# Hybrid decoder layer on one core: small products of a projection slot regrouped, turned values in one tile, first slot's order changed

## The chip, the core and the metric

The kernel runs on one core of one Trainium2 chip. The core has a matrix engine (PE, with its weight loads shown apart as PEld), a vector engine (DVE), a scalar engine (ACT), a third elementwise engine (POOL), and a queue of its own from which most transfers are issued (SP). Products land in a small accumulator memory (PSUM) from which ACT and DVE fetch them. The metric is the device time of one execution in microseconds (us); smaller is better. Three executions of the kernel before took 992.99 us in the median, from 992.9 to 996.05.

## The reference, cut to what matters

One decoder layer over T = 528 rows (16 learned meta tokens and 512 tokens) of width 1024. One projection of the normalised input feeds two mixers with 16 heads of 64 channels each; their outputs are weighed by gates, added, projected, normalised, and go through a feed-forward stage of width 4096.

```
z = layer_norm(concat(meta_tokens, x))          # 528 x 1024
p = z @ w_in                                    # q, k, v of attention, r, k, v and three small inputs of RWKV-7, two gates
# sliding-window attention, 128 keys back, one sink per head, 8 query heads per key head
logits = q k^T / 8 + bias(distance), masked to the window
probs  = exp(logits - m) / (sum exp(logits - m) + exp(sink - m))
att    = probs v
# RWKV-7, per head, S is 64 x 64, step after step
a = sigmoid(a0 + al @ a2);  w = exp(-exp(w(wl)));  g = sigmoid(gl) @ g2
S = S * w_t + (S (-kk_t)) (kk_t a_t)^T + v_t k_t^T
y_t = S r_t
y = (group_norm(y) + bonus) * g
m = sigmoid(gate_a) * att + sigmoid(gate_r) * y
h = deepnorm(z, m @ w_out);  out = deepnorm(h, relu(h @ w1)^2 @ w2)
```

The outputs of the 16 meta rows are dropped at the end.

## The kernel before

**Dense products.** All matrices of weights are multiplied in three steps: the weights and the activations are each split into a high and a low part (ACT makes `whi` at L256, DVE makes `wlo` at L259), and the function `three` (L339 to L342) issues high by high, high by low and low by high into one accumulator bank, `dps`. One unit of dense work is a block of 128 columns of a weight matrix: for 8 blocks of input rows, these three steps, on 264 + 264 columns where all 528 rows are wanted, on 512 where the meta rows aren't. A unit's results are fetched by ACT and DVE (its `evict` function). These fetches run at a raised priority (`ahead(PRI["dense"])`) except inside an aside function that has its own.

**Slots.** The 16 heads are worked on in 8 pairs, and the projection in slots s = -1, 0, ..., 8. A slot holds the dense units of about one pair (names `q`, `k`, `r`, `v`, `ga`, `gr` with the pair's number: queries, keys, reads, values, gate of attention, gate of RWKV) and, between the dense steps, the small products of several pairs at different stages:

- `project_in(s+1)`: the small inputs of the next pair (`rwkv_begin`, `rwkv_lora` twice with accumulator `dps` of the pool `pat`, fetched by ACT at L500, scanned by DVE at L505; `rwkv_sums`, accumulator `ss`, L577).
- `scan(s)`: the pair's scores inside a chunk of 64 steps (`rwkv_scores`, `sc`, L668), the triangular inverse in blocks of 16 on DVE (`rwkv_inverse`, L773 and L777 alternating 15 times, then the copy `Xr` at L778, through DRAM and back as `X` and `XB`), and the transposes (`rwkv_turn_scores`, `rwkv_turn_keys` L729, `rwkv_turn_values` L746).
- `solve(s-1)`: the inverse put together from its blocks (`up` at L820, four levels), folded (`wp` L871, `gq`), the chain of states over 8 chunks (`ch` L946, `Z` on DVE and ACT at L904 and L906), the outputs `Y` (L960) and their norm.
- `attend(s-1)` and `join(s-1)`: the pair's attention, with `sp` (scores, L1131), a softmax on DVE and ACT over `sb`, `pt` (the probabilities transposed, L1169), `av` (L1189), the gate `ga` (L1195), and the sum of both mixers (`merge`).

All of these small products are plain fp32, the dense ones are not. **What sets the order.** The function `weave` walks a list of items `(due time, needs, function)` in order of due time and issues dense steps until the due time has come; the clock of the due times is a count of the dense steps' model durations. So the lists in `scan`, `solve`, `project_in`, `attend` and `join` fix PE's order row by row. The order on DVE, ACT, POOL and SP is set by a scheduler with static priorities at build time, which `ahead(n)` raises for what stands inside it; on the chip each engine runs its own list in order. The accumulator memory is given out as 8 banks: 2 for `dps` of the dense units, 2 of pool `pg` (`sc`, `bp`, `wp`, `gq`, `axt`, `tr`, `vt`, and `ss`), 2 of `pat` (the lora's `dps`, `sp`, `gp`, `pt`, `av`), and one each for `ch` and `Y`. A product that opens a bank waits until the bank's last user has been fetched.

After slot 8 the output projection (L1282 to L1284) and the feed-forward stage (`dps` on 512 columns up, L1501 to L1503 down) follow; the change doesn't touch them.

## Time and profile before

| what | before |
| --- | --- |
| median of three executions | 992.99 us (992.9 to 996.05) |
| profiled execution, its own time | 996.54 us |
| its span in the profile | 994.7 us |
| PE busy | 949.3 us, 95% of the span |
| PEld busy | 790.0 us, 79% |
| DVE busy | 653.1 us, 66% |
| ACT busy | 468.8 us, 47% |
| POOL busy | 44.2 us, 4% |
| mean granted PE clock in the slots | 0.97 to 1.00 |

The span is what the profile records; the execution's own time holds 1.8 us more around it. The profile is one execution, its rows are instructions or groups of them, and a row in square brackets tells how long the engine had stood idle before and what ended that. The count of a group is that of the chip's instructions: a plain fp32 product of the program is two or more of them there. In the trace slot 1 begins at about 114.0 us, slot 2 at 179.5, slot 3 at 243.6, slot 4 at 307.7, and the last slot has ended at 636.

### The profile page before, as it was taken

The page shows a single profiled execution, that of the slowest core. Times are in us where ns is not written, and L with a number is a line of the kernel's source. Part 1 is how long each engine was busy: PE and PEld are TensorE (multiplying, and loading weights), DVE is VectorE, ACT ScalarE, POOL GpSimd, SP SyncE. Part 2 cuts the span into 40 slices and gives each one's busy share as a digit, 9 for nine tenths or more (in the row PEclk, how much of TensorE's full clock was granted, in tenths as well). Part 3 has the DMA queues.
Part 4 walks back from the last instruction along what each step waited for, and adds up shares of the span by engine and source line. Part 5 has one row for each costly group of instructions (what it writes and reads, how often), then busy time and mean ns, then how long its engine had stood idle before and what let it go on. Part 6 is the DMA issues. An engine that isn't in the chain of part 4 may idle for free.

```text
span 994.7 us, 19253 instructions
## 1 busy us (share of the span) xinstructions
PE 949.3 (95%) x7557; PEld 790.0 (79%) x7557; DVE 653.1 (66%) x1505; ACT 468.8 (47%) x1226; POOL 44.2 (4%) x108
## 2 busy tenths in 40 slices
PE   4989899999999999999999999999999999999996
PEld 3989788888888887878886777888888888888885
DVE  8577698787887878778867866766433235443427
ACT  6535448455584575745836833743422224342220
POOL 2000000010010000100001001000000000000001
PEclk9999999999999999999999999999999999999999
DMA  7444432433224432233443536233222232223232
GB/s 270 94 126 120 105 80 69 125 76 105 75 50 123 100 118 68 70 108 88 128 127 103 162 118 229 68 106 116 95 89 102 88 104 88 103 85 106 71 100 84
DMA packets 82674, 105.47 MB, mean 106 GB/s; under 512 B 47766, under 2 KB 54664, under 8 KB 82584
## 3 DMA queue, kind: packets, MB, share of 16 engines
q1 hardware_dynamic: 81088, 102.16, 34.8%
q10 hardware_dynamic: 1496, 2.08, 0.6%
q8 instruction: 59, 0.97, 0.4%
q14 instruction: 31, 0.25, 0.1%
HBM read 86.29 MB, written 13.74 MB: 101 GB/s over the span
## 4 chain that ended last, share of the span: by engine, by line
PE 67%; DVE 17%; ACT 9%; DMA 3%; issue 2%; POOL 0%; SPq 0%; DVEq 0%; ACTq 0%; POOLq 0%
PE dps L340 12%; PE dps L341 11%; PE dps L342 11%; PE acc L1501 6%; PE acc L1503 6%; PE acc L1502 6%; DVE wlo L259 2%; ACT Z L753 2%; PE sc L668 2%; PE av L1189 2%; DVE AX L893 2%; PE o L1282 1%; DVE ftmp L773 1%; DVE Xf L777 1%; PE o L1284 1%
## 5 line engine op out<-in xcount | busy, mean ns | idle before, releaser
L259 DVE TENSOR_TENSOR wlo<-wraw,whi 128x512 fp32r<-128x512 f32 x240 | 158.0, 684 | 176.2 <-ACT whi L256 175.7
L256 ACT CAST whi<-wraw 128x512 fp32r<-128x512 f32 x240 | 140.7, 617 | 275.1 <-PE dps L341 130.6
L340 PE MATMUL dps<-hhi,whi 128*128 128x264 f32 (+1 forms) x640 | 219.3, 343 | 2.5 <-ACT whi L256 1.1
L341 PE MATMUL dps<-hlo,whi 128*128 128x264 f32 (+1 forms) x640 | 205.4, 321 | 1.4 <-DVE hlo L321 1.4
L342 PE MATMUL dps<-hhi,wlo 128*128 128x264 f32 (+1 forms) x640 | 204.2, 319 | 0.4 <-DVE wlo L259 0.4
L340 PEld LDWEIGHTS dps<-hhi,whi 128*128 128x128 f32 x640 | 122.0, 191 | 16.4 <-issue 2.0
L342 PEld LDWEIGHTS dps<-hhi,wlo 128*128 128x128 f32 x640 | 121.8, 190 | 9.1 <-DVE wlo L259 0.6
L341 PEld LDWEIGHTS dps<-hlo,whi 128*128 128x128 f32 x640 | 121.9, 190 | 6.8 <-DVE hlo L321 2.5
L341 PE MATMUL dps<-h1lo,whi 128*128 128x512 f32 (+1 forms) x256 | 97.5, 381 | 0.0
L340 PE MATMUL dps<-h1hi,whi 128*128 128x512 f32 (+1 forms) x256 | 97.4, 381 | 0.0
L342 PE MATMUL dps<-h1hi,wlo 128*128 128x512 f32 (+1 forms) x256 | 97.4, 381 | 0.0
L342 PEld LDWEIGHTS dps<-h1hi,wlo 128*128 128x128 f32 x256 | 48.1, 188 | 10.1
L340 PEld LDWEIGHTS dps<-h1hi,whi 128*128 128x128 f32 x256 | 48.1, 188 | 10.0
L341 PEld LDWEIGHTS dps<-h1lo,whi 128*128 128x128 f32 x256 | 48.1, 188 | 10.0
L1502 PE MATMUL acc<-wlo,hhi 128*128 128x512 f32 x128 | 50.5, 395 | 0.0
L1501 PE MATMUL acc<-whi,hhi 128*128 128x512 f32 x128 | 50.5, 395 | 0.0
L1503 PE MATMUL acc<-whi,hlo 128*128 128x512 f32 x128 | 50.1, 392 | 0.0
L1503 PE MATMUL acc<-whi,flo 128*128 128x512 f32 x112 | 44.0, 393 | 0.0
L1501 PE MATMUL acc<-whi,fhi 128*128 128x512 f32 x112 | 44.0, 393 | 0.0
L1502 PE MATMUL acc<-wlo,fhi 128*128 128x512 f32 x112 | 43.6, 390 | 0.0
L906 ACT ACTIVATE Z<-ch,PC 64x64 f32<-64x64 f32 x56 | 17.3, 309 | 44.8 <-DVE Z L904 43.5
L1601 DVE TENSOR_TENSOR rl<-rl 128x512 f32<-128x512 f32 (+1 forms) x36 | 22.8, 632 | 15.4 <-ACT hhi L1600 9.2
(302 smaller groups left out, 1746.6 us busy)
## 6 DMA issues: line engine op xcount, KB each, us to landing
wraw<-in_w_ff_dram SPq DMA_DIRECT2D x64, 512.0 KB, 3.5
wraw<-in_w_in_dram SPq DMA_DIRECT2D x52, 512.0 KB, 4.1
wraw<-in_w_out_dram SPq DMA_DIRECT2D x8, 512.0 KB, 4.0
xt<-in_x_dram SPq DMA_DIRECT2D x4, 512.0 KB
Nd<-NT SPq DMA_DIRECT2D x16, 128.0 KB, 2.8
bv<-bv SPq DMA_DIRECT2D x8, 256.0 KB
bvm<-bv SPq DMA_DIRECT2D x8, 256.0 KB, 3.7
qs<-qhi SPq DMA_DIRECT2D x16, 128.0 KB, 4.3
```

The lines of the kernel that those rows point to most:

```text
L256: act.copy(hi[:n, qs], raw[:n, qs])
L259: dve.tensor_tensor(lo[:n, qs], raw[:n, qs], hi[:n, qs].bitcast(F32), op=ALU.subtract)
L340: pe.matmul(ps, whi, xhi, start=first, stop=False)
L341: pe.matmul(ps, whi, xlo, start=False, stop=False)
L342: pe.matmul(ps, wlo, xhi, start=False, stop=last)
L668: pe.matmul(scs[e][:, c * P : (c + 1) * P], BK[ER[e], 4 * i + c, :], AXg[ER[e], e, 4 * i + c], start=True, stop=True,)
L753: act.copy(Z[2 * i + cc][64 * (1 - e) : 64 * (1 - e) + 64, e, :], vt[64 * cc : 64 * cc + 64, i * P + e * HD : i * P + (e + 1) * HD],)
L893: dve.tensor_tensor(AXg[:, e, cs], AXg[:, e, cs], gqs[e].rearrange("p (c k t) -> p c k t", c=4, k=2), op=ALU.add,)
L1501: pe.matmul(acc[b], xhi[k][:, bs], hi[:, ws], start=first, stop=False)
L1502: pe.matmul(acc[b], xhi[k][:, bs], lo[:, ws], start=False, stop=False)
L1503: pe.matmul(acc[b], xlo[k][:, bs], hi[:, ws], start=False, stop=last)
L1601: dve.tensor_tensor(r, r, r, op=ALU.mult)
```

## The change

- **Turned values.** `Z` was 8 tiles, filled by 16 copies of 64x64 on ACT in each `rwkv_turn_values`. It is now one tile with the 8 chunks as slices, filled by 4 copies of 64x256.
- **Bank of the sums.** `ss` is opened in pool `pat` and no longer in `pg`.
- **Grouping.** Due times are set so that small products which stood between dense steps each by themselves stand side by side: the sums and the keys' transposes with the outputs (18.6), the values' transposes with the norm (23.2), the lora at 7.4 and 8.6, and the second half of a pair's attention (`attention_turn`, `attention_out`, now in `attend_out`), with the last addition of `merge`, no longer at the end of the slot (26.0 to 31.5) but at the front of the next one (0.0, 4.6, 6.4, 7.0) beside the inverse's products. The product `gp` of the RWKV gate is no part of its dense unit any more but an item (`gate_out`, 11.6), and `merge` is cut in two (`merge_rwkv` at 25.4, `merge`).
- **Priority of fetches.** The queries' fetches (`qhi`, `qlo`) stand inside `ahead(PRI["dense"])`. In slot 0 the inverse's steps on DVE stand inside `ahead(PRI["up"])`.
- **Order of units.** In slot 0 the queries go ahead of the next pair's keys. In slots 1 to 6 the RWKV gate goes ahead of the attention gate. In slot 7 the order becomes RWKV gate, queries, attention gate, and the last two gates.

```diff
...
 AHEAD = 2
-NBUF = {'AX': 2, 'BK': 1, 'NT': 2, 'GR': 2, 'Z': 8}
+NBUF = {'AX': 2, 'BK': 1, 'NT': 2, 'GR': 2}
...
         pool.memset(dvm, 1.0)
-        ss = pg.tile([P, 512], F32, name="ss", tag="g")
+        ss = pat.tile([P, 512], F32, name="ss", tag="a")
...
         v = S["v"]
-        Z = [rw.tile([P, 2, HD], F32, name=f"Z{c}", tag="Z", bufs=NBUF["Z"]) for c in range(NCH)]
-        S["Z"] = Z
+        Z = rw.tile([P, NCH, 2, HD], F32, name="Z", tag="Z")
+        S["Z"] = [Z[:, c] for c in range(NCH)]
...
                 )
-            for i in range(4):
-                for cc in range(2):
-                    for e in range(2):
-                        act.copy(
-                            Z[2 * i + cc][64 * (1 - e) : 64 * (1 - e) + 64, e, :],
-                            vt[64 * cc : 64 * cc + 64, i * P + e * HD : i * P + (e + 1) * HD],
-                        )
+            v4 = vt.rearrange("p (i e h) -> p e i h", i=4, e=2)
+            for cc in range(2):
+                for e in range(2):
+                    act.copy(
+                        Z[64 * (1 - e) : 64 * (1 - e) + 64, cc::2, e, :],
+                        v4[64 * cc : 64 * cc + 64, e],
+                    )
...
         pool.memset(Xf.rearrange("p a b -> p (a b)")[:, 0 :: B + 1], 1.0)
-        for s in range(B - 1):
-            nj, nt = s + 1, B - 1 - s
-            tv = tmp[:, 0 : nj * nt].rearrange("p (j t) -> p j t", j=nj)
-            dve.tensor_tensor(
-                tv, Xf[:, 0:nj, s : s + 1].to_broadcast([NB, nj, nt]),
-                Nf[:, s : s + 1, s + 1 :].to_broadcast([NB, nj, nt]), op=ALU.mult,
-            )
-            dve.tensor_tensor(Xf[:, 0:nj, s + 1 :], Xf[:, 0:nj, s + 1 :], tv, op=ALU.add)
-        dve.tensor_copy(Xr, Xf[0:64].rearrange("p a b -> p b a"))
+        with ahead(PRI["up"] if j == 0 else 0):
+            for s in range(B - 1):
+                nj, nt = s + 1, B - 1 - s
+                tv = tmp[:, 0 : nj * nt].rearrange("p (j t) -> p j t", j=nj)
+                dve.tensor_tensor(
+                    tv, Xf[:, 0:nj, s : s + 1].to_broadcast([NB, nj, nt]),
+                    Nf[:, s : s + 1, s + 1 :].to_broadcast([NB, nj, nt]), op=ALU.mult,
+                )
+                dve.tensor_tensor(Xf[:, 0:nj, s + 1 :], Xf[:, 0:nj, s + 1 :], tv, op=ALU.add)
+            dve.tensor_copy(Xr, Xf[0:64].rearrange("p a b -> p b a"))
...
         def evict(ps, t0, n):
-            act.activation(hi, ps, AF.Copy, scale=HD**-0.5)
-            dve.scalar_tensor_tensor(
-                lo, ps, HD**-0.5, hi.bitcast(F32), op0=ALU.mult, op1=ALU.subtract
-            )
+            with ahead(PRI["dense"]):
+                act.activation(hi, ps, AF.Copy, scale=HD**-0.5)
+                dve.scalar_tensor_tensor(
+                    lo, ps, HD**-0.5, hi.bitcast(F32), op0=ALU.mult, op1=ALU.subtract
+                )
...
+        A["gw", j] = gwh, gwl
         yield from dense(COL_GRW + j * P, XT_, evict)
+    def gate_out(j):
         gp = pat.tile([P, 512], F32, name="gp", tag="a")
-        three(gp, gwh, gwl, sghi, sglo)
+        three(gp, *A["gw", j], sghi, sglo)
...
         dve.scalar_tensor_tensor(t, t, 1.0, gp, op0=ALU.add, op1=ALU.mult)
-        yield 0.7
...
-    def merge(j):
+    def merge_rwkv(j):
...
         dve.tensor_tensor(z, z, A["gg", j], op=ALU.mult)
+    def merge(j):
+        z = SS[j]["z"]
...
     unit("av", COL_AV, aside_value())
+    query(0)
...
     reads(1)
-    query(0)
...
     for j in range(1, PAIRS - 1):
+        gate_rwkv(j - 1)
         gate_att(j - 1)
-        gate_rwkv(j - 1)
...
     j = PAIRS - 1
+    gate_rwkv(j - 1)
+    query(j)
     gate_att(j - 1)
-    query(j)
-    gate_rwkv(j - 1)
...
             (12.4, (), F(rwkv_turn_scores, j)),
-            (19.0, (), F(rwkv_turn_keys, j)),
+            (18.6, (), F(rwkv_turn_keys, j)),
             (16.0, (), F(rwkv_inverse_place, j)),
-            (21.4, (), F(rwkv_turn_values, j)),
+            (23.2, (), F(rwkv_turn_values, j)),
...
             (18.6, (), F(rwkv_outputs, j)),
-            (24.5, (), F(rwkv_norm, j)),
+            (23.2, (), F(rwkv_norm, j)),
...
             (0.0, (), F(rwkv_begin, j)),
-            (5.6, (), F(rwkv_lora, j, 0)),
-            (7.4, (), F(rwkv_lora, j, 1)),
-            (20.4, (f"k{j}",), F(rwkv_sums, j)),
+            (7.4, (), F(rwkv_lora, j, 0)),
+            (8.6, (), F(rwkv_lora, j, 1)),
+            (25.5 if j == 1 else 18.6, (f"k{j}",), F(rwkv_sums, j)),
...
-    def attend(j, t0=9.2, t1=26.0):
+    def attend(j, t0):
+        return [(t0, (f"q{j}",), F(attention_scores, j, 0))] + [
+            (t0 + t, (), F(attention_scores, j, 1 + i)) for i, t in enumerate((0.0, 2.8, 4.4))
+        ]
+    def attend_out(j, t0, t1, t2):
         return [
-            (t0, (f"q{j}",), F(attention_scores, j, 0)),
-            (t0, (), F(attention_scores, j, 1)),
-            (t0 + 2.8, (), F(attention_scores, j, 2)),
-            (t0 + 4.4, (), F(attention_scores, j, 3)),
-            (t1, (), F(attention_turn, j, 0)),
-            (t1 + 2.4, (), F(attention_out, j, 0)),
-            (t1 + 2.4, (), F(attention_turn, j, 1)),
-            (t1 + 4.8, (f"ga{j}",), F(attention_out, j, 1)),
+            (t0, (), F(attention_turn, j, 0)),
+            (t1, (), F(attention_out, j, 0)),
+            (t1, (), F(attention_turn, j, 1)),
+            (t2, (f"ga{j}",), F(attention_out, j, 1)),
...
-    def join(j, t2):
-        return [(t2, (f"gr{j}",), F(merge, j))]
+    def join(j, t0, t1, t2):
+        return [
+            (t0, (f"gr{j}",), F(gate_out, j)), (t1, (), F(merge_rwkv, j)), (t2, (), F(merge, j)),
+        ]
...
             if 0 < s < PAIRS - 1:
-                items += attend(s - 1) + join(s - 1, 31.5)
+                items += attend(s - 1, 9.2) + join(s - 1, 11.6, 25.4, 0)[:2]
+            if 1 < s < PAIRS:
+                items += attend_out(s - 2, 0.0, 4.6, 6.4) + join(s - 2, 0, 0, 7.0)[2:]
...
                 items += [(10.0, (), merged_before)]
-                items += attend(s - 1, t1=20.5) + join(s - 1, 26.5)
-                items += attend(s, 16.5)[:4]
+                items += attend(s - 1, 10.0) + attend_out(s - 1, 20.5, 22.9, 25.3)
+                items += join(s - 1, 11.6, 26.5, 26.5)
+                items += attend(s, 16.5)
...
             if s == PAIRS:
-                items += attend(s - 1, t1=3.0)[4:] + join(s - 1, 25.5)
+                items += attend_out(s - 1, 3.0, 5.4, 7.8) + join(s - 1, 0.0, 24.5, 25.5)
...
                 items += [(3.0 + 3 * b, (), F(residual_rows, b)) for b in range(4)]
```

**PE, the outputs in slot 2** (slots 1 to 6 alike; `dps` are the dense steps, `Y` the outputs, `tr` the transposed keys, `ss` the sums of the next pair). Before:

```order
L960 MATMUL Y<-Z_2098,AX 64x64
L960 MATMUL Y<-Z_2099,AX 64x64
L340 MATMUL dps<-hhi,whi 128x264
L341 MATMUL dps<-hlo,whi 128x264
L342 MATMUL dps<-hhi,wlo 128x264
L729 MATMUL tr<-con,BK 128x128 x8
L340 MATMUL dps<-hhi,whi 128x264
```

Now:

```order
L962 MATMUL Y<-Z,AX 64x64 x16
L729 MATMUL tr<-con,BK 128x128 x8
L577 MATMUL ss<-con,sq 64x2 x8
L578 MATMUL ss<-con,sq 16x2
L340 MATMUL dps<-hhi,whi 128x264
L341 MATMUL dps<-hlo,whi 128x264
L342 MATMUL dps<-hhi,wlo 128x264
```

The dense steps between `Y` and `tr` stand behind them now, and `ss`, which stood between dense steps of its own, follows `tr` at once.

**DVE, the front of slot 3** (`L` is the scan of the next pair's decay, `WT` the folded matrix, `Xf` and `ftmp` the steps of the inverse, `ga` and `z` the gate on attention and the sum of the mixers). Before:

```order
L611 TENSOR_TENSOR bv<-bp,v 128x512
L259 TENSOR_TENSOR wlo<-wraw,whi 128x512
L505 SCALAR_TENSOR_TENSOR L<-con,tw 128x528
L875 TENSOR_TENSOR WT<-wp,dv 128x512 x2
L773 TENSOR_TENSOR ftmp<-Xf,Nf 66x15
L777 TENSOR_TENSOR Xf<-Xf,ftmp 66x15
```

Now:

```order
L877 TENSOR_TENSOR WT<-wp,dv 128x512
L779 TENSOR_TENSOR Xf<-Xf,ftmp 66x15
L775 TENSOR_TENSOR ftmp<-Xf,Nf 66x28
L1200 SCALAR_TENSOR_TENSOR ga<-ga,av 128x512
L779 TENSOR_TENSOR Xf<-Xf,ftmp 66x2x14
L1215 TENSOR_TENSOR z<-z,ga 128x512
L775 TENSOR_TENSOR ftmp<-Xf,Nf 66x39
L779 TENSOR_TENSOR Xf<-Xf,ftmp 66x3x13
L775 TENSOR_TENSOR ftmp<-Xf,Nf 66x48
L779 TENSOR_TENSOR Xf<-Xf,ftmp 66x4x12
L775 TENSOR_TENSOR ftmp<-Xf,Nf 66x55
L505 SCALAR_TENSOR_TENSOR L<-con,tw 128x528
```

The scan `L`, which stood ahead of `WT` and of the inverse, stands behind `WT`, the first steps of the inverse, and `ga` and `z`. These two belong to the pair before, and stood at the end of the slot before.

**DVE, the inverse of pair 0 in slot 0** (`BK`, `u` are operands of the pair's scores). Before:

```order
L777 TENSOR_TENSOR Xf<-Xf,ftmp 66x11x5
L554 TENSOR_TENSOR BK<-kp,iP 64x8x64
L773 TENSOR_TENSOR ftmp<-Xf,Nf 66x48
L554 TENSOR_TENSOR BK<-kp,iP 64x8x64
L777 TENSOR_TENSOR Xf<-Xf,ftmp 66x12x4
L540 SCALAR_TENSOR_TENSOR u<-ta,k 128x528
L773 TENSOR_TENSOR ftmp<-Xf,Nf 66x39
L550 SCALAR_TENSOR_TENSOR BK<-u,drv,iP 64x8x64
L777 TENSOR_TENSOR Xf<-Xf,ftmp 66x13x3
```

Now:

```order
L775 TENSOR_TENSOR ftmp<-Xf,Nf 66x55
L779 TENSOR_TENSOR Xf<-Xf,ftmp 66x11x5
L775 TENSOR_TENSOR ftmp<-Xf,Nf 66x48
L779 TENSOR_TENSOR Xf<-Xf,ftmp 66x12x4
L775 TENSOR_TENSOR ftmp<-Xf,Nf 66x39
L779 TENSOR_TENSOR Xf<-Xf,ftmp 66x13x3
```

The steps of the inverse follow each other now; the products of other work that stood between them come later.

## The prediction

> **What bounds the kernel now.** I read the page first, then the table by stage, then what PE waits for, then PE's timeline around the small products. The page has PE busy for 95% of the span:
>
> ```profile
> span 994.7 us, 19253 instructions
> PE 949.3 (95%) x7557; PEld 790.0 (79%) x7557; DVE 653.1 (66%) x1505; ACT 468.8 (47%) x1226; POOL 44.2 (4%) x108
> ```
>
> So there is room for 45 us at most without making PE's own work shorter. The table by stage (window, length, then the busy time of PE, PEld, DVE, ACT, POOL, the granted clock, the DMA share, GB/s) shows one middle slot and the feed-forward stage:
>
> ```profile
> 243.60:307.70 64.10, 62.74 (x692) 52.83 (x695) 51.69 (x138) 38.45 (x117) 3.92 (x10) 1.00 0.34 94
> 636.00:994.00 358.00, 350.75 (x1585) 287.29 (x1583) 160.78 (x250) 110.19 (x202) 3.69 (x4) 1.00 0.28 93
> ```
>
> A slot lasts 64.1 us, PE is idle for 1.4 of them, and DVE for 12.4. The last 358 us hold no line of the change; I leave them as they are. What the change can move is PE's idle time in the slots, and what PE loses when it passes from dense steps to small products and back, which the profile books as busy. The waits of PE that it touches (total, times, mean):
>
> ```profile
> PE av L1189 <- DVE pown L1175: 4.9, 5, 1.0
> PE up L820 <- DMA X<-Xr: 3.6, 1, 3.6
> PE pt L1169 <- ACT sb L1159: 1.5, 1, 1.5
> PE sc L668 <- DVE AX L685: 1.1, 2, 0.6
> PE axt L708 <- DVE Xf L777: 0.7, 3, 0.2
> ```
>
> **The change part by part. A, fewer passages.** PE's timeline in slot 3 (start, duration) shows a lone `ch`, and `Y` and `tr` with dense steps between them:
>
> ```profile
> 280.02 0.28 PE L342 MATMUL dps<-hhi,wlo 128*128 128x264 f32 x1
> 280.24 0.34 PE L946 MATMUL ch<-Z,AX 128*64 128x64 f32 x4
> 280.50 0.39 PE L340 MATMUL dps<-hhi,whi 128*128 128x264 f32 x1
> 280.73 0.28 PE L341 MATMUL dps<-hlo,whi 128*128 128x264 f32 x1
> ...
> 281.58 0.28 PE L342 MATMUL dps<-hhi,wlo 128*128 128x264 f32 x1
> 281.79 1.15 PE L960 MATMUL Y<-Z,AX 128*64 128x64 f32 x32
> 282.87 0.39 PE L340 MATMUL dps<-hhi,whi 128*128 128x264 f32 x1
> 283.10 0.29 PE L341 MATMUL dps<-hlo,whi 128*128 128x264 f32 x1
> 283.22 0.29 PE L342 MATMUL dps<-hhi,wlo 128*128 128x264 f32 x1
> 283.35 1.03 PE L729 MATMUL tr<-con,BK 128*128 128x128 f32 x8
> 284.14 0.37 PE L340 MATMUL dps<-hhi,whi 128*128 128x264 f32 x1
> 284.34 0.28 PE L341 MATMUL dps<-hlo,whi 128*128 128x264 f32 x1
> ```
>
> Dense steps start 0.12 us apart (283.10 to 283.22). From the step before `ch` to `ch` it is 0.22, so entering costs 0.10; from the step behind it to the next 0.23, so leaving costs 0.11: 0.21 in all. For `Y` the same reading gives 0.09 and 0.11, for `tr` 0.01 and 0.08, together 0.29. In slot 7 these two stand side by side already, between steps of 512 columns (0.12 x 512/264 = 0.23 apart):
>
> ```profile
> 540.70 0.40 PE L342 MATMUL dps<-hhi,wlo 128*128 128x512 f32 x1
> 541.03 1.15 PE L960 MATMUL Y<-Z,AX 128*64 128x64 f32 x32
> ...
> 542.96 0.48 PE L340 MATMUL dps<-hhi,whi 128*128 128x512 f32 x1
> 543.28 0.39 PE L341 MATMUL dps<-hlo,whi 128*128 128x512 f32 x1
> ```
>
> Entering costs 0.10, leaving 0.09, and the two products take 1.93 (541.03 to 542.96) against 1.08 + 0.79 = 1.87 apart. So joining them saved 0.29 - 0.19 - 0.06 = 0.04. In the order of PE's instructions, stretches of plain fp32 products between dense steps fall from 181 to 152, by 29. Each is worth 0.04 (a whole-array transpose beside a narrow product) to 0.21 (a stretch like `ch` that vanishes into its like, as the two loras do, or `av` beside the narrow products of the inverse): -1.2 to -6.1 us. Both kinds are there in about equal number, so I take the middle, 0.13 each: **-3.8**.
>
> [...]
>
> **B and C, the attention's second half.** `av` followed its `pt` so closely at the slot's end that `pown`, made by DVE from `pt`, came late five times: 4.9 us. In the new order the first `av` has 27 dense steps between it and `pt`, over 3 us at 0.12 each, and the second has nine dense steps and other products; the mean wait is 1.0. I take the wait as gone: **-4.9** (0 to -4.9; without that cover it comes back at the front). The one wait of `pt` for `sb` in slot 6 goes the same way, since `pt` now comes in the slot after `sb`: **-1.5** (0 to -1.5).
>
> **D, the seam from slot 0 to slot 1.** DVE's, SP's and PE's timelines there:
>
> ```profile
> 105.47 0.38 DVE L778 COPY Xr<-Xf 64x256 f32<-64x256 f32 x1
> 108.27 0.59 SPq L781 DMA_DIRECT2D Xr<-Xr  x1
> 110.32 0.63 SPq L790 DMA_DIRECT2D X<-Xr  x1
> 113.32 0.73 PE L820 MATMUL up<-X,NT 16*32 16x16 f32 x64 [3.63 <-DMA X<-Xr]
> ```
>
> The copy is done at 105.85, but its transfer is issued only at 108.27, behind the queries' transfers on SP; from there to `up` it takes 5.05 (113.32 - 108.27). PE was ready at 113.32 - 3.63 = 109.69. With the queries a unit earlier, their transfers are out before, so even with the copy unmoved `up` could start at 110.9, a wait of 1.2. With the inverse's steps in one piece on DVE the copy comes some us earlier still, and the wait is gone: -3.6. What these steps now push back on DVE are the operands of pair 0's scores; a late `AX` cost `sc` 1.1 us in its two waits, and I charge that once: **-2.5** (0 to -3.6).
>
> **E.** `axt` waits three times, 0.2 each, until DVE's list has passed a step of the inverse; the attention's products now stand ahead of it on PE and give DVE that time: **-0.7** (0 to -0.7).
>
> **F, the copies of `Z`.** ACT's groups (busy, mean ns):
>
> ```profile
> L753 ACT COPY Z<-vt 64x64 f32<-64x64 f32 x128 | 26.4, 206 | 9.0 <-PE vt L746 7.6
> L733 ACT COPY GR<-tr 64x256 f32<-64x256 f32 x32 | 11.7, 364 | 1.3 <-PE tr L729 1.2
> ```
>
> The 32 new copies have the size of the `GR` copies: 11.7 us where 26.4 were. These 14.7 us lie on an engine that is busy for 47%, beside dense steps; nobody waits for `Z` until the next slot's chain. With that cover gone (a dense fetch queued behind it on ACT) it would be up to -1. I take **0** (0 to -1).
>
> **G, a new wait at the front of slots 2 to 6.** These stand now behind the attention's half. The rows of slot 3 before, DVE, ACT and PE:
>
> ```profile
> 259.25 1.26 DVE L505 TENSOR_TENSOR_SCAN L<-con,tw 128x528 f32<-128x528 f32 x1 [0.63 <-ACT tw L503]
> 260.43 1.26 DVE L875 TENSOR_TENSOR WT<-wp,dv 128x512 f32<-128x512 f32 x2
> 260.54 0.22 ACT L512 ACTIVATE Pm<-L 128x16 f32<-128x16 f32 x1 [1.32 <-DVE L L505]
> 261.91 0.84 ACT L500 ACTIVATE ta<-dps,drv 128x264 f32<-128x264 f32 x2
> 264.66 0.28 PE L1131 MATMUL sp<-khi,qs 128*128 128x256 f32 x1
> 298.99 0.44 PE L1189 MATMUL av<-pown,vdif 128*64 128x128 f32 x4 [0.97 <-DVE pown L1175]
> ...
> 299.80 0.44 PE L1169 MATMUL pt<-con,sb 128*128 128x128 f32 x2
> ```
>
> Twelve products of `av` take 0.81 (298.99 to 299.80), so both halves of 16 take 2.2, and the two `pt` about 1.0 more by the same pace: 3.2 us move ahead of `sp`, which comes to 264.66 + 3.2 = 267.9. `sp` opens a bank of `pat` that the second lora's first half holds until ACT has made `ta`, and `ta` stands behind `Pm`, `Px` and `iP` on ACT, which wait for the scan `L`. The lora is due 1.8 us later and 3.2 us of work stand ahead of it: `L` would start at 264.25. But DVE's list now has `ga` and `z` ahead of `L`, each of the size of one `WT` (0.63): it starts at about 265.5 and ends 1.26 later, at 266.75. `ta` began 1.4 behind the end of `L` (260.51 to 261.91), and its first half takes 0.42: the bank is free at 268.6, and PE waits 0.7, in each of five slots: **+3.5**. Were DVE on time it is 0; with one scan's duration (1.3) more, for instance behind a late `ftmp`, it is 2.0 x 5 = +10. Behind `sp` on PE everything of the slot is queued, so nothing gives this back. I take 0.7, the reading by rows.
>
> **H, slot 7.** The queries come second there, so their transfers stand behind the inverse's two on SP, 0.59 and 0.63 in the rows under D, and the scores of pair 6 or 7 may wait for them: **+1.2** (0 to +5, a wait like that of D with its 5.05 queue).
>
> The sum: -3.8 - 4.9 - 1.5 - 2.5 - 0.7 + 0 + 3.5 + 1.2 = **-8.7**. The profiled execution took 996.54 (its span 994.7 and 1.8 around it), so it would become 987.8. It was 3.5 us above the median of the runs, 992.99, whose own spread to the slowest run is 3.1. I take the difference off the median: **984.3 us**.
>
> **The rivals.** *No new wait:* the ends of A (-6.1) and D (-3.6) with B, C and E, and G and H at 0: -16.8, 976.2 us. For it: DVE has 12.4 us idle in a slot, and the scheduler may leave `L` enough room. Against it: DVE's order puts `ga` and `z` right before `L`.
>
> *Joining is worth nothing:* each stretch saves 0.04, as in slot 7, A is -1.2, the rest stands: -6.1, 986.9 us. For it: slot 7, the one place where the profile shows a joined stretch. Against it: the loras join their like.
>
> *Slower, by the chain at the front:* `L` (1.26), the exponentials (1.4) and `ta` (0.42) lie bare, 3.1 us in five slots, +15.5 instead of +3.5: 996.3 us. It decides from (8.7 + 3.5)/5 = 2.4 us of wait in a slot. For it: steps of three engines in a row, and two banks of `pat`; against it: dense steps stand between, and DVE would have to be 2.4 us later than read.
>
> *The waits only move:* `av` then waits at the front as it did at the end, `pt` too, and the seam waits for another transfer: B, C and D are 0 and the sum is +0.2, 993.2 us. Against it: the cover under B.
>
> **How the numbers follow.** Forecast 0.46, with its own range of 980 to 989; no new wait 0.20; joining worth nothing 0.17; slower 0.09; waits only move 0.08. About 0.3%, 3 us, is what a measurement of this kernel tells from no change, so faster ends at 990 and slower begins at 996. Faster: 0.45 + 0.20 + 0.16 = 0.81; slower 0.06 of the third rival and 0.01 of the last; the rest, 0.12, is the same. The range from 975 to 992 holds the forecast, the first two rivals nearly whole, and leaves out most of the last two.
>
> **What would show it.** A: PE's busy time in a slot like 243.6 to 307.7 falls by about 0.6 with its count of passages; if it falls by 0.2, joining is worth nothing. B, C: no row of `av` waiting for `pown`, none of `pt` for `sb`. D: no wait of `up` for `X`, or a row of `sc` in its place. G: a new row of `sp` waiting for ACT's `ta`, five times 0.7; if it is missing, the first rival, if it is above 2.4, the third. H: in slot 7 a wait of `sp` for the transfer `qs`. The forecast is wrong if the slots' period stays at 64.1 us.

## The result and the profile after

The changed kernel takes **984.34 us** in the median of four runs (983.99 to 987.41), the kernel before 993.61 on the same chip; the ratio is 0.9903, with a 95% interval from 0.9882 to 0.9924. The number of the forecast, 984.3, was met, and it lay in the range. Its sum was not met: two of its largest terms were wrong, and the largest single cause of the gain stood in it at nothing. The experiments found that out.

The page of the changed kernel (span, and busy time of each engine):

```profile
span 982.3 us, 19147 instructions
PE 940.8 (96%) x7557; PEld 787.7 (80%) x7557; DVE 655.2 (67%) x1505; ACT 455.7 (46%) x1130; POOL 47.8 (5%) x108
```

What PE waits for in it (total, times, longest; the third figure of the prediction's list is the longest wait too):

```profile
PE ch L948 <- ACT Z L908: 3.4, 5, 1.4
PE dps L340 <- DVE qlo L1072: 2.8, 6, 0.5
PE sp L1136 <- ACT ta L500: 2.7, 4, 0.7
PE vp L1052 <- ACT ta L500: 1.5, 1, 1.5
PE sp L1136 <- DVE sb L1139: 1.2, 1, 1.2
PE sc L668 <- DVE AX L685: 1.0, 2, 0.6
PE pt L1174 <- ACT sb L1164: 0.4, 1, 0.4
```

The waits of `av` for `pown` (4.9), of `up` for `X` (3.6) and of `axt` are gone. `sp` waits for `ta` as the forecast read it, 0.67 in four slots, and in slot 5 `vp` stands in its place with 1.47. In slot 1 `vp` waits another 1.47, for which the profile names no engine. A wait that no step of the forecast had is new: a dense step at the end of each of six slots waits 0.48 for `qlo`, where before there was one of 0.4.

The table by stage of the change, a middle slot and slot 7, in the columns of the prediction's table:

```profile
231.20:294.60 63.40, 62.24 (x687) 53.12 (x688) 51.84 (x138) 36.68 (x105) 4.28 (x10) 1.00 0.33 92
487.30:548.90 61.60, 58.51 (x621) 45.66 (x620) 48.02 (x127) 33.69 (x99) 2.86 (x3) 1.00 0.45 126
```

A middle slot takes 63.40 instead of 64.10. Slot 7, from its first `up` to the next, grew from 59.1 to 61.6, because the second half of one more pair's attention stands in it; slot 1 has that half less.

### The profile page after: what moved, and what is told of

Read it like the earlier page. It is cut to its first block, busy times and chain, and to the rows that moved or that the text cites. A ratio compares the mean times of both kernels' runs of the same rounds, so it can differ in the third digit from the quotient of the medians.

```text
span 982.3 us, 19147 instructions
## 1 busy us (share of the span) xinstructions
PE 940.8 (96%) x7557; PEld 787.7 (80%) x7557; DVE 655.2 (67%) x1505; ACT 455.7 (46%) x1130; POOL 47.8 (5%) x108
## 4 chain that ended last, share of the span: by engine, by line
PE 72%; DVE 17%; ACT 4%; DMA 2%; issue 2%; POOL 2%; SPq 0%; DVEq 0%; ACTq 0%
PE dps L340 12%; PE dps L341 11%; PE dps L342 11%; PE acc L1516 6%; PE acc L1518 6%; PE acc L1517 6%; DVE wlo L259 3%; PE sc L668 2%; PE o L1290 1%; PE av L1194 1%; PE ch L948 1%; PE wp L873 1%; PE o L1291 1%; PE o L1292 1%; POOL grs L971 1%
## 5 line engine op out<-in xcount | busy, mean ns | idle before, releaser
L340 PE MATMUL dps<-hhi,whi 128*128 128x264 f32 (+1 forms) x640 | 216.5, 338 | 4.5 <-DVE qlo L1072 2.8
L342 PE MATMUL dps<-hhi,wlo 128*128 128x264 f32 (+1 forms) x640 | 203.0, 317 | 0.4 <-DVE wlo L259 0.4
L340 PEld LDWEIGHTS dps<-hhi,whi 128*128 128x128 f32 x640 | 120.5, 188 | 19.4 <-DVE qlo L1072 4.1
L342 PEld LDWEIGHTS dps<-hhi,wlo 128*128 128x128 f32 x640 | 120.5, 188 | 9.0 <-DVE wlo L259 0.6
L340 PE MATMUL dps<-h1hi,whi 128*128 128x512 f32 (+1 forms) x256 | 97.5, 381 | 0.0
L342 PE MATMUL dps<-h1hi,wlo 128*128 128x512 f32 (+1 forms) x256 | 97.5, 381 | 0.0
L342 PEld LDWEIGHTS dps<-h1hi,wlo 128*128 128x128 f32 x256 | 48.1, 188 | 10.3
L340 PEld LDWEIGHTS dps<-h1hi,whi 128*128 128x128 f32 x256 | 48.1, 188 | 10.1
L908 ACT ACTIVATE Z<-ch,PC 64x64 f32<-64x64 f32 x56 | 17.3, 310 | 36.4 <-DVE Z L906 35.7
```

Of the source, the lines that this page charges most:

```text
L340: pe.matmul(ps, whi, xhi, start=first, stop=False)
L342: pe.matmul(ps, wlo, xhi, start=False, stop=last)
L908: act.activation(dst, src[ER[e]], AF.Copy, scale=scale)
```

## The experiments

Twelve more runs were made, one of them of the kernel before, in four groups on several chips; each has the kernel before beside it on its own chip, with medians of 996.1 to 997.4 there. The change itself ran only beside the 993.6 of its own chip, so rows of different groups are compared by their ratios. "Waits" is the sum of all listed waits of PE that end between 60 and 640 us, and "dips" is the time lost to a lower granted clock in the same stretch (last section but one); both are from the one profiled execution.

| kernel | median us | ratio to before (95%) | middle slot | waits | dips |
| --- | --- | --- | --- | --- | --- |
| before, first profile | 993.6 | | 64.07 | 20.2 | 5.1, and 1.7 before 60 |
| before, second profile | 993.4 (one run) | | 64.07 | 18.8 | 5.1 |
| the change | 984.3 | 0.9903 (0.9882 to 0.9924) | 63.4 | 17.3 | 0 |
| change, attention at the slot's end | 991.7 | 0.9961 (0.9943 to 0.9979) | 64.3 | 20.9 | 3.4 |
| change, loras in the other order | 984.7 | 0.9892 (0.9851 to 0.9933) | 63.4 | 17.0 | 1.7 |
| change, loras early | 986.4 | 0.9895 (0.9870 to 0.9919) | 64.4 | 16.7 | 1.7 |
| change, 16 copies | 996.5 | 0.9999 (0.9977 to 1.0022) | 64.0 | 23.2 | 8.5 |
| change, stretches apart | 986.8 | 0.9896 (0.9872 to 0.9921) | 63.0 | 18.1 | 1.7 |
| change, queries of slot 0 back | 993.7 (one run) | | 63.3 | 20.7 | 8.5 |
| before, 4 copies | **981.3** | 0.9843 (0.9816 to 0.9870) | 62.6 | 10.3 | 3.4 |
| before, 4 copies, stretches joined | 986.5 | 0.9913 (0.9880 to 0.9948) | 63.5 | 14.8 | 3.4 |
| before, 4 copies, ACT held longer | 996.7 (one run) | | 63.6 | 20.2 | 6.8 |
| before, 4 copies, slot 0's order | 980.6 | 0.9845 (0.9820 to 0.9870) | 62.7 | 9.1 | 3.4 |
| the same, sums of pair 1 late | 981.2 | 0.9843 (0.9822 to 0.9864) | 62.7 | 10.1 | 1.7 |

**The kernel before again.** No edit.

> The kernel before, unchanged, for a second profile. The first one had a granted clock of 0.91 in 20 to 40 us and in 60 to 80 us and of 0.97 in 100 to 150 us, and took 996.54 us beside a median of 993. If the clock is what made it longer, this profile has 1.00 in these windows, a span of about 991, slot 1 beginning at about 110 instead of 113.3, and the same waits: av for pown five times about 1.0, up for X about 3.6, and a period of 64.1 us in slots 2 and 3. If the length is not the clock's, slot 1 begins at 113.3 again with the clock at 1.00.

One run took 993.41 with a span of 991.6. Slot 1 began at 110.18 and not at 113.32, while the waits in the slots and the period of 64.07 came again to 0.02 us. The clock was not at full speed all along, though: it was low at other places (0.51, 0.50 and 0.50 in the windows of 2 us from 60, 112 and 488 us). Ahead of slot 1 the waits did differ: two of `sc` for `AX` (1.1 together) and one of 0.3 between 70 and 74 us came in the first profile only. With the 1.7 us more that the clock lost there, they make up the 3.1 us between the two spans. So the waits in the slots repeat, and the two profiles differ in length by the clock and by the waits ahead of slot 1.

**The 16 copies back in the change.**

```diff
-            for cc in range(2):
-                for e in range(2):
-                    act.copy(Z[64 * (1 - e) : 64 * (1 - e) + 64, cc::2, e, :], v4[64 * cc : 64 * cc + 64, e])
+            for i in range(4):
+                for cc in range(2):
+                    for e in range(2):
+                        act.copy(Z[64 * (1 - e) : 64 * (1 - e) + 64, 2 * i + cc, e, :], v4[64 * cc : 64 * cc + 64, e, i])
```

> The change with one part undone: 16 copies of 64x64 for turned values instead of 4 of 64x256, into the one tile. By my theory they lie off the path: ACT's busy time rises by 13 to 15 us and the time stays within 1 us of the change (984.3). The rival, that merged copies are the gain (queries' and dense fetches stand behind them on ACT), expects +3 us or more, with new waits of PE for whi, qlo or sb.

996.52 us: the whole gain was gone, and my theory of these copies with it. A middle slot took 64.0, as before the change. PE's waits of that kernel:

```profile
PE dps L340 <- DVE qlo L1073: 6.9, 6, 1.2
```

The wait for `qlo` is 1.15 in each slot instead of 0.48, because `qhi` stands on ACT behind the copies: in slot 2 fifteen of them run from 226.28 to 229.53 us, and `qhi` begins at 230.07. In the profiles, 5.9 us of the loss are waits (23.2 against 17.3), and the clock lost 8.5 where it lost nothing in the change.

**The 4 copies alone.** After that the question was whether the copies need the rest of the change. The kernel before, with one tile for `Z` and the 4 copies, and nothing else:

```diff
-        Z = [rw.tile([P, 2, HD], F32, name=f"Z{c}", tag="Z", bufs=NBUF["Z"]) for c in range(NCH)]
-        S["Z"] = Z
+        Z = rw.tile([P, NCH, 2, HD], F32, name="Z", tag="Z")
+        S["Z"] = [Z[:, c] for c in range(NCH)]
...
+            for cc in range(2):
+                for e in range(2):
+                    act.copy(Z[64 * (1 - e) : 64 * (1 - e) + 64, cc::2, e, :], v4[64 * cc : 64 * cc + 64, e])
```

> The kernel before with one part of the change alone: turned values in one tile with 4 copies. In the changed kernel 16 copies cost 0.67 us a slot, as a longer wait of dense steps for qlo. By my theory that is so because the change took the attention's products from the slot's end and PE comes to the last dense unit sooner than ACT and DVE; in the kernel before nobody waits there, so this part alone gives nothing: ACT's busy time falls by 13 to 15 us, slots 2 and 3 stay at 64.1, within 1 us of the kernel before. The rival, that the copies stand in ACT's way in both kernels, expects 63.4 to 63.5 a slot and -4 us.

It took 981.33 us, ratio 0.9843: faster than the whole change, and the intervals of the two ratios don't touch. I had expected no gain, and the rival 4 us. A middle slot takes 62.6. The rows show how. Before, ACT and DVE near the end of slot 3:

```profile
289.31 3.48 ACT L753 COPY Z<-vt 64x64 f32<-64x64 f32 x16 [0.39 <-PE vt L746]
292.69 0.40 ACT L1159 ACTIVATE sb<-sb,sm 128x128 f32<-128x128 f32 x1
293.11 0.48 ACT L421 ACTIVATE r<-dps,drv 128x264 f32<-128x264 f32 x1
293.63 0.22 DVE L415 SCALAR_TENSOR_TENSOR r<-edge,vc,r 128x1 f32<-128x1 f32 x1 [1.85 <-ACT r L421]
...
298.25 0.68 DVE L1175 TENSOR_TENSOR pown<-pt,con 128x512 f32<-128x512 f32 x1
```

With the 4 copies alone, the same places in slot 4, ACT, DVE and PE:

```profile
344.55 1.50 ACT L753 COPY Z<-vt 64x256 f32<-64x256 f32 x4 [0.43 <-PE vt L746]
345.96 0.40 ACT L1159 ACTIVATE sb<-sb,sm 128x128 f32<-128x128 f32 x1
346.39 0.48 ACT L421 ACTIVATE r<-dps,drv 128x264 f32<-128x264 f32 x1
346.91 0.22 DVE L415 SCALAR_TENSOR_TENSOR r<-edge,vc,r 128x1 f32<-128x1 f32 x1
351.89 0.68 DVE L1175 TENSOR_TENSOR pown<-pt,con 128x512 f32<-128x512 f32 x1
352.96 0.39 PE L1189 MATMUL av<-pown,vdif 128*64 128x128 f32 x4
```

`r` on ACT is a dense unit's fetch. From the start of the copies to it, 3.80 us pass before and 1.84 now. Before, DVE stands idle for 1.85 us and waits for it; with the 4 copies DVE doesn't wait there at all. All that DVE has queued behind `r` moves up with it: from the start of the copies to `pown` it is 8.94 before and 7.34 now. So `av` finds `pown` ready, and its wait, five times 0.97, is gone without moving the attention. Here are PE's dense steps on either side of the longest stretch of `av` and `pt`, two lines before and two with the 4 copies:

```profile
297.26 0.39 PE L342 MATMUL dps<-hhi,wlo 128*128 128x512 f32 x1
300.21 0.37 PE L340 MATMUL dps<-hhi,whi 128*128 128x264 f32 x1
352.37 0.39 PE L342 MATMUL dps<-hhi,wlo 128*128 128x512 f32 x1
354.13 0.37 PE L340 MATMUL dps<-hhi,whi 128*128 128x264 f32 x1
```

From step to step this stretch takes 2.95 before and 1.76 now. The three stretches of `pt` and `av` of a slot, read in this way, take 5.0 before and 3.6 now. These 1.44 us are the whole of what a middle slot gains, and some 0.5 of them stood in no row of PE's own waits but in PE's busy time. The weight loads show where: those of `av` waited 7.2 for `pown` in the kernel before, 2.3 more than its products. Besides, the wait of `pt` for `sb` in slot 6 falls from 1.55 to less than 0.15, and at the seam `up` waits 1.4 for `X` where it waited 3.6.

**ACT held longer.** Behind the 4 copies, 8 copies of pieces of the tile onto themselves; the values stay as they are.

```diff
+            for cc in range(2):
+                for e in range(2):
+                    for u in range(2):
+                        zs = Z[64 * (1 - e) : 64 * (1 - e) + 64, cc + 4 * u : cc + 4 * u + 3 : 2, e, :]
+                        act.copy(zs, zs)
```

> The kernel before with the 4 copies, and behind them on ACT 8 copies of pieces of the tile onto themselves (64x128, values unchanged), which hold ACT for about 2 us more but no bank of the accumulator. If ACT's time is what the 16 copies cost (r's fetch and the softmax's scaling queue behind them, then DVE, then pown, then av), av waits for pown again, about 1.0 in each slot, and a middle slot is back at 64. If it was the bank of vt or the form of the tile that mattered, it stays at 62.6.

One run, 996.65; a middle slot is 63.6, two thirds of the way back from 62.6 to 64.07, and the waits are at 20.2:

```profile
PE pt L1174 <- ACT sb L1164: 4.7, 6, 1.5
PE up L825 <- DMA X<-Xr: 3.7, 1, 3.7
```

The wait came back at `pt` for `sb` and not at `av` for `pown`: four of these copies stand ahead of `r` and four behind it, ahead of the softmax's scaling of `sb`. So the expectation missed the place. It did tell the causes apart: ACT's time is what counts, since the accumulator bank and the tile are those of the fast kernel.

**The attention back at the slot's end.**

```diff
-                items += attend(s - 1, 9.2) + join(s - 1, 11.6, 25.4, 0)[:2]
-            if 1 < s < PAIRS:
-                items += attend_out(s - 2, 0.0, 4.6, 6.4) + join(s - 2, 0, 0, 7.0)[2:]
+                items += attend(s - 1, 9.2) + join(s - 1, 11.6, 25.4, 31.5)
+                items += attend_out(s - 1, 26.0, 28.4, 30.8)
```

> The change with one part undone: the second half of a pair's attention and the last addition of merge go back to the end of the slot (26.0, 28.4, 30.8, 31.5) in slots 1 to 6. By my theory the av waits come back (5 or 6 times 1.0, +5), the waits of sp and vp for ta go (4 x 0.67 and 1.5, about -4.2), and 18 passages come back at 0.13 each (+2.3): about +3 us, 987.5. The rival that the wait moved with the attention (nothing gained by moving it) expects no av waits to come back, or the same time within 1 us. The rival that joining is worth nothing (0.04 a passage) expects +1.5, 986.

991.7 us, 7 more than the change, where I expected 3. The `av` waits came back, six of 0.7:

```profile
PE sp L1136 <- ACT ta L500: 4.4, 4, 2.4
PE av L1194 <- DVE pown L1180: 4.4, 6, 0.7
```

Two things follow. With the later due times of the change (values at 23.2 instead of 21.4) `av` is late again although there are only 4 copies, so there the attention has to move. And `sp` still waits for `ta`: 0.67 in three slots and 2.38 in one. The 3.2 us of attention ahead of `sp` don't make that wait; the later due times of the loras do, as the early loras below show.

**The loras in the other order, and early.** Two edits aimed at that wait. The first:

```diff
-            (7.4, (), F(rwkv_lora, j, 0)),
-            (8.6, (), F(rwkv_lora, j, 1)),
+            (7.4, (), F(rwkv_lora, j, 1)),
+            (8.6, (), F(rwkv_lora, j, 0)),
```

> The change with the two small products of rwkv_lora in the other order: ta's at 7.4, tw's at 8.6, so that ta no longer stands on ACT behind Pm, Px and iP, which wait for the scan L. By my theory of the new wait, the waits of sp (4 x 0.67) and of vp (1.5, perhaps twice) go: -3 to -5.5 us, about 980. A rival reads the wait as one for the bank itself, held by any second lora: then sp waits for tw instead, 0.5 or more each, and the time stays within 1 us of the change. A second rival: the scan L comes 1 us later and the wait turns up at the keys' products of the pair, time 984 to 986.

984.73 us, the same as the change, where I expected 980. The wait for `ta` is gone, but the sum of waits is hardly lower:

```profile
PE ch L948 <- ACT Z L908: 5.5, 5, 1.4
PE dps L340 <- DVE qlo L1072: 2.9, 6, 0.5
PE sp L1136 <- DVE Xf L779: 1.4, 1, 1.4
```

The chain of states takes it over, with 0.94 where it had none in the middle slots. The other edit puts the loras earlier:

```diff
-            (7.4, (), F(rwkv_lora, j, 0)),
-            (8.6, (), F(rwkv_lora, j, 1)),
+            (5.6, (), F(rwkv_lora, j, 0)),
+            (7.4, (), F(rwkv_lora, j, 1)),
```

> The change with the two lora products due at 5.6 and 7.4 as before, two stretches of small products fewer. The waits of sp for ta stayed when the attention went back to the slot's end, so they seem to come from the later due times. By that theory they go here (0.67 a slot, 1.5 where vp waited) and nothing takes their place, since the scan L is early on DVE: a middle slot is 62.7 and the time 980. The rival, from the run with the two in the other order, is that the wait turns up in the chain (ch for Z, 0.9): 63.4 a slot and 984.

986.42 us, a middle slot 64.4: the second lora's product now waits for `tw` (3.3 in five slots), `ch` for `Z` (6.2 in all) and the wait for `qlo` stays. The rival was right in kind, and the time came out above both expectations. So the front of the slot has several chains of nearly the same length, and in both runs to take away one wait there was worth nothing.

**Stretches apart, and stretches joined.** Four due times of the change put back as before, and the same four put into the kernel with 4 copies:

```diff
-            (18.6, (), F(rwkv_turn_keys, j)),
-            (23.2, (), F(rwkv_turn_values, j)),
-            (23.2, (), F(rwkv_norm, j)),
-            (25.5 if j == 1 else 18.6, (f"k{j}",), F(rwkv_sums, j)),
+            (19.0, (), F(rwkv_turn_keys, j)),
+            (21.4, (), F(rwkv_turn_values, j)),
+            (24.5, (), F(rwkv_norm, j)),
+            (25.5 if j == 1 else 20.4, (f"k{j}",), F(rwkv_sums, j)),
```

> The change with four due times as before, so that outputs, keys' transposes, sums, values' transposes and norm stand between dense steps each by themselves again: 19 stretches more, 3 in a slot; all else as changed. By the price of the prediction (0.13 each) a middle slot gets 0.4 us longer (63.8 instead of 63.4) and the time rises by 2.5. At 0.21, which the attention put back suggested (3 stretches, 0.62 us), a middle slot is 64.0 and the time +4. The rival that joining is worth 0.04 expects 63.5 and +0.8. If the waits for qlo (0.48 in each slot) go with it, 0.5 a slot comes off.

For the second kernel the diff is read from its plus lines to its minus lines, on the kernel before with 4 copies, and `ss` is opened in `pat` as in the change; the sums stood at 20.4 for every pair there.

> The kernel before with the 4 copies, and outputs, keys' transposes and sums side by side (18.6), values' transposes and norm side by side (23.2), ss in the other pool: 20 stretches of small products fewer, attention and lora where they were. If a stretch saves 0.13, a middle slot falls from 62.6 by 0.4 to 62.2 and the time by 2.6 to 978.7. If it saves 0.04 or nothing, as outputs, keys and sums side by side (3.46 us in the change against 3.50 to 3.58 apart) and values and norm (1.34 against 1.33) suggest, the slot stays within 0.15 of 62.6; if the sums and values bunched on ACT and DVE make a new wait, it is above 62.6.

With three stretches more a slot, a middle slot became shorter, 63.0 instead of 63.4, where every price that I had put on a stretch made it longer. Of that, 0.22 is a shorter wait for `qlo` (0.26), and PE's busy time fell as well:

```profile
233.66:296.62 62.96, 62.03 (x684) 53.07 (x683) 51.62 (x138) 36.35 (x105) 3.91 (x10) 1.00 0.34 89
```

The median, 986.75, is above the change's 984.3, though the intervals of the ratios overlap nearly whole. It is where the price of 0.13 would have it, but for another reason: slot 1 begins 2.7 later there, with one dip of 1.7 and a wait of `vt` of 0.7 ahead of it. Joined in the faster kernel, the stretches cost 5 us: the values' copies come later, and `av` waits again:

```profile
PE av L1189 <- DVE pown L1175: 3.4, 6, 0.8
```

The table by stage says what passages are worth. The kernel with 4 copies alone, a middle slot:

```profile
298.80:361.40 62.60, 62.20 (x687) 52.83 (x687) 51.93 (x138) 36.66 (x105) 4.20 (x12) 1.00 0.38 101
```

PE is busy for 62.20 in it with four stretches more than the change has in a slot, for 62.24 in the change, and for 62.74 in the kernel before, which has as many stretches as the first. The joined stretch in the change, in slot 3:

```profile
273.23 0.28 PE L342 MATMUL dps<-hhi,wlo 128*128 128x264 f32 x1
273.44 1.15 PE L962 MATMUL Y<-Z,AX 128*64 128x64 f32 x32
274.52 1.09 PE L729 MATMUL tr<-con,BK 128*128 128x128 f32 x8
275.54 1.09 PE L577 MATMUL ss<-con,sq 128*64 128x2 f32 x16
276.56 0.20 PE L578 MATMUL ss<-con,sq 128*16 128x2 f32 x2
276.70 0.39 PE L340 MATMUL dps<-hhi,whi 128*128 128x264 f32 x1
276.93 0.28 PE L341 MATMUL dps<-hlo,whi 128*128 128x264 f32 x1
```

From the step before it to the second step behind it pass 3.70 us; less two dense steps (0.24) it costs 3.46, where the three apart cost 1.28 + 0.88 + 1.42 = 3.58 in the kernel before: 0.06 for each of the two passages saved. `tr` takes 1.02 inside (274.52 to 275.54) and took 0.79 alone, so of some 0.35 saved at the edges 0.23 is paid between the products.

**The queries of slot 0 back behind the keys.**

```diff
-    query(0)
     keys(1)
     reads(1)
+    query(0)
```

> The change with the queries of slot 0 behind the next pair's keys and reads again; the inverse of pair 0 keeps its priority on DVE. If the early copy Xr is enough, slot 1 begins at 105 as in the change. If the order of the transfers on SP is what made X late, up waits for X again, 1 to 3.6 us, and slot 1 begins at 106 to 109. If the granted clock in 60 to 80 us hangs on the order of the units, it is 0.91 there again as in both profiles of the kernel before, and slot 1 begins 1.5 later.

The wait came back in full. DVE's copy `Xr`, with the raised priority, is done at 102.4; SP and PE:

```profile
102.40 0.62 SPq L1081 DMA_DIRECT2D qs<-qhi  x1
103.58 0.47 SPq L1081 DMA_DIRECT2D qs<-qlo  x1
104.10 0.59 SPq L1081 DMA_DIRECT2D qs<-qhi  x1
104.74 0.59 SPq L1081 DMA_DIRECT2D qs<-qlo  x1
105.38 0.59 SPq L783 DMA_DIRECT2D Xr<-Xr  x1
110.38 0.30 PE L822 MATMUL up<-X,NT 16*32 16x16 f32 x8 [3.55 <-DMA X<-Xr]
```

Its transfer stands behind the four of the queries, and `up` waits 3.55 as before the change. So it takes the order of the units to remove the wait, as the forecast's term D read it, and the inverse's priority on DVE alone does nothing for it; the order without the priority wasn't run. The listed waits between 60 and 115 us, which hold the seam, are 4.8 in the second profile of the kernel before and 2.0 in the change, 1.0 of it the two of `sc` for `AX` that D charged. The clock in 60 to 80 us was low here (0.91) as in both profiles of the kernel before (0.91 each). But it was low there too in the kernel with the stretches apart, which has the queries early (0.58 and 0.57 in the windows of 2 us from 72 and 74 us), and full, 1.00, in the one with ACT held longer, which has them late; so it doesn't hang on that order.

**A faster kernel.** The 4 copies with slot 0's order (unit order, raised fetches of queries, inverse ahead), everything else as before:

```diff
-    keys(1)
-    reads(1)
     query(0)
+    keys(1)
+    reads(1)
...
+        with ahead(PRI["up"] if j == 0 else 0):
             for s in range(B - 1):
...
+            with ahead(PRI["dense"]):
                 act.activation(hi, ps, AF.Copy, scale=HD**-0.5)
```

> The kernel before with three parts of the change: turned values in one tile with 4 copies, the queries of slot 0 ahead of the next pair's keys (with their fetches at raised priority), and the inverse of pair 0 ahead on DVE. Attention, loras, sums, gates and due times stay as before. With the copies alone up still waited 1.4 for X and a dense step 1.0 for qlo in slot 0. By my theory these two go and the middle slots stay at 62.6: 2 to 3.5 us less than the copies alone (981.3), so 978 to 979, faster than both kernels. The rival, that raised fetches of queries bring the waits for qlo at the end of every slot, expects 63.1 a slot and 982.

980.57 us, ratio 0.9845, where I expected 978 to 979. `up` doesn't wait and two of three middle slots stay at 62.7 (one takes 64.0), but `ss` waits 1.42 for `AX` on ACT in slot 0.

The change has the sums of pair 1 at 25.5 in that slot, so I took that over too:

> The kernel with copies and slot 0's order (980.6), and one due time more from the change: the sums of pair 1 at 25.5 instead of 20.4 in slot 0, where ss waited 1.42 us for the copy AX on ACT. If that wait is all that kept the seam's gain, slot 1 begins 1.4 earlier than there (at the same granted clock) and the time is about 979. The rival, that slot 0's wait only moves (to X or to a dense step), expects the same start of slot 1 and 980.5.

```diff
-            (20.4, (f"k{j}",), F(rwkv_sums, j)),
+            (25.5 if j == 1 else 20.4, (f"k{j}",), F(rwkv_sums, j)),
```

981.21 us. The wait of `ss` is gone, and another stands in its place, as the rival had it, though in slot 1: `sc` waits 1.90 for `d` on DVE.

The two and the 4 copies alone can't be told apart by their times (980.6, 981.2, 981.3, on different chips). By their ratios all three are faster than both kernels of this case. Not tried by themselves are the bank of `ss`, the gates' order and `gate_out`.

## Why the prediction was right, and where it was wrong

The time was right, and so was the sign. The working was not: the steps have to be held to the runs one by one.

| step | said | measured |
| --- | --- | --- |
| A, fewer passages | -3.8 | about 0: PE's busy time in a slot 62.24 with four stretches fewer, 62.20 without; 62.03 with three apart again |
| B, `av` for `pown` | -4.9, by the attention's move | gone, 4.9 and some 2.5 in weight loads; the 4 copies alone do the same |
| C, `pt` for `sb` | -1.5 | gone from slot 6; also with the 4 copies alone |
| D, seam | -2.5 | -2.8 in the waits from 60 to 115 us |
| E, `axt` | -0.7 | gone |
| F, copies of `Z` | 0 | alone -8.5 in waits, 12.3 by the spans (991.6 to 979.3, 1.7 of it fewer dips); without them the change gains nothing |
| G, front of slots 2 to 6 | +3.5 | +4.2, and 1.5 in slot 1, but the wait moves when removed |
| H, slot 7 | +1.2 | no wait for `qs`; `ch` for `Z` 1.44 where it was 0.84 |
| not in it: `qlo` at a slot's end | | +2.5 |
| not in it: the clock | | 6.8 and 5.1 lost in the two profiles before, nothing in the change up to 640 us |

**The step that failed is F.** It said that the copies lie on an engine busy for 47% beside dense steps, and that nobody waits for `Z` until the next slot's chain. Both are so. But `r`'s fetch and the softmax's scaling of `sb` stand behind the copies on ACT, DVE stood idle 1.85 us for that fetch, and `pown` and then `av` came late by it. The step named this cover ("a dense fetch queued behind it on ACT") and priced its loss at no more than 1 us without following that fetch to DVE. The row for `r` on DVE, idle for 1.85 us ahead of it for ACT, was in the trace of the kernel before, 5 us ahead of the `av` wait that stood in the list.

So **B** had the right wait and the wrong cure: I took the wait's name, `pown`, for its cause, and the distance between `pt` and `av` for what was missing. With 4 copies and the old due times the distance is as before and the wait is gone. In the changed kernel the attention's move is needed only because the change's later due times bring the wait back, and it costs the wait for `qlo` at the slot's end, which with the attention back is a single one of 0.2.

**A** was mis-sized: 0.13 for a stretch, where the whole of a slot's four was within 0.04 us. Its count was high too: stretches between the steps of L340 to L342 go from 197 to 174 in the two traces, by 23 and not 29. The sign that the prediction named for it, 0.6 less of PE's busy time in a slot, did nearly come (62.74 to 62.24), but it isn't A's: the 4 copies alone bring it with no stretch joined, by what the products of `pt` and `av` no longer lose. The lone `ch`, the dearest passage (0.21), isn't among the stretches that the change removes. The one joined stretch that the trace showed, in slot 7, gave 0.04, and the second rival stood on it; I took the middle between two ends where one of them had no instance. Inside the joined stretch of `Y`, `tr` and `ss` two thirds of the edges' saving, 0.23 of some 0.35 us, are paid again.

**G** had the right size in the right place, four times 0.67, by a chain of which one link was wrong: the due time of the loras, not the attention's 3.2 us, brings `sp` so close behind `ta`. Taking it away wins nothing: the chain of states waits instead.

Why the number came out nevertheless: the waits that PE shows between 60 and 640 us fell by 1.5 (18.8 to 17.3, with the second profile of the kernel before), about 2.5 more lay in the weight loads of `av`, and that profile lost 5.1 us to the clock where the change lost none. Together that is 9.1, where the two spans differ by 9.3. The forecast's terms without A come to -4.9, near the 4.0 of the first two parts; in the place of A's 3.8 stands the clock, for which the forecast had no term. That the two are of nearly the same size, and the number came out to a tenth, is luck.

Of the rivals, the second (joining is worth nothing) described A; the fourth (the waits only move) was right about the parts of the change other than the copies: with 16 copies the change took 996.5 against 996.4 of the kernel before.

## What the runs showed of the hardware

**The granted clock went to 0.50 for 3.4 us at a time, mostly at a wait of PE of more than 1 us.** In windows of 2 us the low clock of the kernel before has this form, behind the wait of 3.63 us for `X`, which ended at 113.32:

```profile
114.00:116.00 2.00, 2.00 (x27) 1.67 (x22) 0.08 (x1) 0.52 (x2) 0.00 (x0) 0.72 0.93 358
116.00:118.00 2.00, 2.00 (x5) 1.61 (x6) 1.96 (x5) 0.00 (x0) 0.00 (x0) 0.50 0.08 27
118.00:120.00 2.00, 2.00 (x73) 1.45 (x72) 0.94 (x2) 0.02 (x1) 0.00 (x0) 0.93 0.00 0
```

0.28, 0.50 and 0.07 of 2 us are missing: 1.7 us of full clock, so 3.4 us at half. In windows of 0.2 us the clock of this dip is 0.69 from 114.8, 0.50 in each from 115.0 to 118.2, 0.78 in the next, and 1.00 from 118.4 on. All other dips up to 640 us, in all kernels, are 1.7 us too, or 3.4 and in one place 5.1. From 60 us on most begin within or soon behind a wait of PE of more than 1 us; three follow only shorter ones, as that at 73.9 us of the kernel before, behind two of 0.56 and 0.58. The dips of the table are these sums; one more at the very end, behind PE's last product, isn't counted (in the change it is 0.50 from 977 us on). In the change with 16 copies one follows the wait of `vp` that ended at 128.38 after 1.48 us:

```profile
128.00:130.00 2.00, 1.62 (x11) 1.46 (x12) 2.00 (x7) 2.00 (x5) 0.00 (x0) 0.91 0.00 0
130.00:132.00 2.00, 2.00 (x9) 1.90 (x9) 1.37 (x6) 0.06 (x1) 0.00 (x0) 0.50 0.21 66
132.00:134.00 2.00, 2.00 (x11) 1.34 (x12) 1.05 (x5) 0.56 (x2) 0.00 (x0) 0.73 0.00 0
```

and in the change itself none follows the same wait (1.47, ended at 127.84), nor four others of 1.1 to 1.5 us from there to 640 us:

```profile
128.00:130.00 2.00, 2.00 (x16) 1.80 (x16) 1.72 (x7) 1.53 (x4) 0.00 (x0) 1.00 0.04 12
130.00:132.00 2.00, 2.00 (x16) 1.46 (x16) 2.00 (x10) 0.61 (x2) 0.00 (x0) 1.00 0.16 54
```

So a wait of 1.5 us had a dip behind it in one run and none in another. What makes the difference was not tested, nor was it shown that the wait is the cause. A part of the spread of the runs may come from such dips: of the change's runs the slowest, 987.41, has the lowest mean granted clock, 0.994, but those of 983.99 and 984.06 have 0.995 and 0.997.

Whether the 16 copies lower the clock by anything but these waits stays open. Over their runs the mean granted clock of the kernel before and of the change with 16 copies was 0.986 to 0.995; that of the change with the attention put back, with 4 copies and almost as many waits (20.9 against 23.2), was 0.992 to 0.998.

## What to carry to other kernels

An engine at 47% is not off the path in the 3.5 us in which a burst stands ahead of a fetch: look at what is queued behind the burst on its own engine, and follow that to the next engine's idle rows, before its cost is put at nothing. A wait's row names the one that came last; its cause is found by going back along the engine named, until a row shows it idle. And behind some waits of a busy matrix engine the clock was at half for 3.4 us, 1.7 us lost on top of the wait, so compare two kernels with their waits and their clock apart.
